# Two-layer attention block on Trainium2: at the layer boundaries, five tiles of squares summed by the matmul engine and the residual add moved to the vector engine

## The chip, the cores and the metric

The kernel runs on one core of one Trainium2 chip. The metric is device microseconds of one execution, as the median of several runs. A core has a matmul engine (TensorE, PE in the profile), a vector engine (VectorE, DVE), an activation engine (ScalarE, ACT), a general-purpose engine (GpSimd, POOL), a sequencer that issues most transfers (SyncE, SP), and DMA engines. Each engine works through its own queue in order, and waits on semaphores for the others.

## The reference, cut to what matters

Two layers work on a residual stream `x` of 512 tokens by 1024 channels. The two places in a layer at which the stream is updated look like this:

```python
mixed = (gate[..., :D_MODEL] * y_nsa + gate[..., D_MODEL:] * y_sb) @ w_out
x = x + rms_norm(mixed, norm_g[1])
hf = rms_norm(x, norm_g[2])
ff = jnp.square(jax.nn.relu(hf @ w_ff1)) @ w_ff2
return x + rms_norm(ff, norm_g[3])
```

Each update needs the sum of squares of the branch's result over all 1024 channels, then the residual add, then the sum of squares of the new `x` for the norm ahead of the next matrix.

## The kernel before, in words

The stream is kept transposed: channels lie on the 128 partitions in eight tiles (`KT` = 8) and the 512 tokens lie along a row. Every f32 product is made of three passes over split operands (`three`, lines 183 to 187): high weight by high activation, high by low, low by high. A `Weight` (lines 145 to 177) is loaded by a transfer that SP issues, its high part is rounded off on ACT (`w_hi`, line 157) and the rest subtracted on POOL (`w_lo`, line 162). There are two buffers for raw weights and four for split ones, so a new split waits until PE has left an older weight.

The code around the change is `tail` (lines 242 to 337). It runs four times: after `w_out` and after the second feed-forward matrix in each layer. In three of these a next matrix follows (`nxt` is set); these are the boundaries of this text, called 1, 2 and 3 in order of time. The fourth is the end of the kernel. At a boundary the tokens are cut in two halves of 256 (`HALVES`).

- The first three tiles of the result have been made and their squares summed over the whole row before `tail` starts. The last five (`GN` = 5) are made in `tail`, first for half 0, then for half 1 (`products`, `evacuate`).
- `evacuate` copies a product out of PSUM on DVE (line 261, or line 263 where a partial sum is added), squares it on ACT into a buffer `sq`, and adds the square on DVE to the accumulator `acc` (`sq_add`, lines 229 to 237; called `macc` or `facc` in the profile). `sq` has two buffers.
- `rstd_fin` (lines 209 to 222) multiplies `acc` with a matrix of ones on PE (line 212). This sums over partitions and leaves the sum on all of them (`ss`). ACT and DVE then make the reciprocal root (`Rpost`, or `Rpre` for the norm of the next matrix). The multiplication is f32, which the trace shows as two PE passes.
- `residual` (lines 282 to 296) handles the eight tiles: DVE scales a tile (`pn`, line 291), POOL adds the old `x` (line 292), ACT makes the high part `ah` of the next matrix's input and DVE the low part `al` (`xsplit`, lines 224 to 227).
- `squares` (lines 298 to 303) squares the new `x` on ACT and sums on DVE into `acc2`.
- `head_step` (lines 200 to 203) multiplies the new inputs with the next matrix's first four column tiles, one input tile after the other.

PE's order is the program's order. At a boundary it is: half 0 of the five tiles; tile 0 of half 1; `ss` of half 0; tiles 1 to 4 of half 1; `head_step` on half 0 for input tiles 0 and 1; `ss` of half 1; `head_step` on half 0 for tiles 2 to 7; `head_step` on half 1 for tiles 0 to 5; `ss` of the new `x`, half 0; tile 6; `ss` of the new `x`, half 1; tile 7; then the next stage. The order on the other engines is set when the program is built: a list scheduler takes, from the instructions that are ready by its own estimate of time, the one that comes first in the program. On the chip each queue then runs in that fixed order. In that program order `residual` of half 0 stands ahead of `evacuate` of the tiles 1 to 4 of half 1.

Of the kernel before, what the change touches and what calls it, by code (L numbers as in the profile page):

```python
# [8 lines left out]
F32 = mybir.dt.float32  # L9
F32R = mybir.dt.float32r  # L10
I32 = mybir.dt.int32
AF = mybir.ActivationFunctionType
ALU = mybir.AluOpType
# [12 lines left out]
P = 128  # L26
# [23 lines left out]
def layer_kernel(ctx, tc, xT, pos, gvec, tri, consts, smalls, w_in, w1, w_o, w_out, ff1, ff2, out):  # L50
    nc = tc.nc
    V, S, G, E = nc.vector, nc.scalar, nc.gpsimd, nc.tensor

    cp = ctx.enter_context(tc.tile_pool(name="cp", bufs=1))
    sp = ctx.enter_context(tc.tile_pool(name="sp", bufs=1))
# [6 lines left out]
    def big(tag, name, dt=F32):  # L62
        return sp.tile([P, T], dt, tag=tag, bufs=BUFS[tag], name=name)

    def half(name):
        return sp.tile([P, 256], F32, tag="sv", bufs=3, name=name)

    def psum(tag, name):
        return pp.tile([P, T], F32, tag=tag, bufs=2, name=name)
# [10 lines left out]
    x = [big("L", f"x{k}") for k in range(KT)]  # L80
# [8 lines left out]
    ones = cp.tile([P, P], F32, name="ones")  # L89
# [99 lines left out]
    def dense(ps, w, acts, k0=0):  # L189
        n = len(acts)  # L190
        for k in range(n):
            three(ps, w, k0 + k, acts[k], k == 0, k == n - 1)

    HALVES = (slice(0, 256), slice(256, 512))
    FULL = (slice(0, 512),)

    def cols(acts, c):
        return [(h[:, c], l[:, c]) for h, l in acts]

    def head_step(group, acts, c, ks):  # L200
        for k in ks:
            for ps, w in group:
                three(ps[:, c], w, k, (acts[k][0][:, c], acts[k][1][:, c]), k == 0, k == KT - 1)

    def gcol(l, n, k):
        c = (l * 4 + n) * KT + k
        return gv[:, c:c + 1]

    def rstd_fin(R, acc, c, more=None, tag="t"):
        n = c.stop - c.start  # L210
        ss = psum(tag, "ss")[:, 0:n]
        E.matmul(ss, ones, acc, start=True, stop=more is None)
        if more is not None:
            E.matmul(ss, ones, more, start=False, stop=True)
        v = half("var")
        y = R[:, c]
        S.activation(y, ss, AF.Ln, scale=1.0 / D, bias=eps_c)
        V.tensor_scalar(v, ss, 1.0 / D, EPS, ALU.mult, ALU.add)
        S.activation(y, y, AF.Exp, scale=-0.5)
        V.tensor_tensor(acc, y, y, ALU.mult)  # L220
        V.scalar_tensor_tensor(v, acc, -0.5, v, ALU.mult, ALU.mult)
        V.scalar_tensor_tensor(y, v, 1.5, y, ALU.add, ALU.mult)

    def xsplit(act, xk, g, c):
        h, l = act[0][:, c], act[1][:, c]
        S.activation(h, xk[:, c], AF.Copy, scale=g)
        V.scalar_tensor_tensor(l, xk[:, c], g, h.bitcast(F32), ALU.mult, ALU.subtract)

    def sq_add(acc, src, first, c, eng):
        n = c.stop - c.start  # L230
        if first:
            S.activation(acc, src, AF.Square)
        else:
            for o in range(0, n, 256):
                sq = sp.tile([P, 256], F32, tag="sq", bufs=2, name="sq")
                S.activation(sq, src[:, o:o + 256], AF.Square)
                eng.tensor_tensor(acc[:, o:o + 256], acc[:, o:o + 256], sq, ALU.add)

    def new_acts():
        return [(big("act", f"ah{k}", F32R), big("act", f"al{k}", F32R)) for k in range(KT)]  # L240

    def tail(l, n, mixed, acc, load, acts, prev, src, nxt, head):


        group = range(KT - GN, KT)
        last_sq = []
        na = new_acts() if nxt is not None else None
        R = big("R", "Rpost")
        R2 = big("R", "Rpre") if nxt is not None else None
        ws = [load(m, ("f", "w", "w", "w", "pt")[i]) for i, m in enumerate(group)]  # L250
        pst = [psum(("d", "s", "o", "o", "s")[i], f"tail{m}") for i, m in enumerate(group)]

        def products(hf, i):
            c = HALVES[hf]
            dense(pst[i][:, c], ws[i], cols(acts, c))

        def evacuate(hf, i):
            c = HALVES[hf]
            m, ps = group[i], pst[i][:, c]
            if prev is None:  # L260
                V.tensor_copy(mixed[m][:, c], ps)
            else:
                V.tensor_tensor(mixed[m][:, c], ps, prev[m][:, c], ALU.add)
            if nxt is None and (hf, i) == (1, GN - 1):
                last_sq.append(half("last_sq"))
                S.activation(last_sq[0], mixed[m][:, c], AF.Square)
            else:
                sq_add(acc[:, c], ps if prev is None else mixed[m][:, c], False, c, V)
            if nxt is None and hf == 1:
                S.activation(mixed[m][:, c], mixed[m][:, c], AF.Copy, scale=gcol(l, n, m))  # L270

        def old(hf):
            if src is None:
                return [x[k][:, HALVES[hf]] for k in range(KT)]
            r = []
            for j in range(4):
                t = big("sig", "x_old").rearrange("p (a t) -> p a t", a=2)
                nc.sync.dma_start(t, src[:, 2 * j:2 * j + 2, HALVES[hf]])
                r += [t[:, 0, :], t[:, 1, :]]
            return r  # L280

        def residual(hf, xo):
            c = HALVES[hf]
            for k in range(KT):
                t = big("t", "pn")[:, 0:256]
                if nxt is None and hf == 1:
                    e = G if k in ENDP else V
                    e.tensor_tensor(t, mixed[k][:, c], R[:, c], ALU.mult)
                    (G if k == 5 else e).tensor_tensor(x[k][:, c], t, xo[k], ALU.add)
                else:  # L290
                    V.scalar_tensor_tensor(t, mixed[k][:, c], gcol(l, n, k), R[:, c], ALU.mult, ALU.mult)  # L291
                    (V if nxt is None and k in (1, 4, 7) else G).tensor_tensor(x[k][:, c], t, xo[k], ALU.add)
                if nxt is not None:
                    xsplit(na[k], x[k], gcol(nxt[0], nxt[1], k), c)
                else:
                    nc.sync.dma_start(out[:, k, c], x[k][:, c])

        def squares(hf):
            c = HALVES[hf]
            acc2 = half("acc2")  # L300
            for k in range(KT):
                sq_add(acc2, x[k][:, c], k == 0, c, V)
            return acc2

        for i in range(GN):
            products(0, i)
            evacuate(0, i)
        xo = old(0)
        if src is not None:
            for k in range(KT):  # L310
                x[k] = big("L", f"x{k}")
        products(1, 0)
        rstd_fin(R, acc[:, HALVES[0]], HALVES[0])
        evacuate(1, 0)
        hd = head.start() if nxt is not None else None
        residual(0, xo)
        for i in range(1, GN):
            products(1, i)
            evacuate(1, i)
        xo = old(1)  # L320
        if nxt is None:
            for m in range(KT - GN):
                S.activation(mixed[m][:, HALVES[1]], mixed[m][:, HALVES[1]], AF.Copy, scale=gcol(l, n, m))
            rstd_fin(R, acc[:, HALVES[1]], HALVES[1], last_sq[0])
            residual(1, xo)
            return None
        head_step(hd, na, HALVES[0], (0, 1))
        rstd_fin(R, acc[:, HALVES[1]], HALVES[1])
        residual(1, xo)
        a2 = squares(0), squares(1)  # L330
        head_step(hd, na, HALVES[0], range(2, KT))
        head_step(hd, na, HALVES[1], range(PLAN["HS"]))
        rstd_fin(R2, a2[0], HALVES[0])
        head_step(hd, na, HALVES[1], range(PLAN["HS"], PLAN["HS2"]))
        rstd_fin(R2, a2[1], HALVES[1])
        head_step(hd, na, HALVES[1], range(PLAN["HS2"], KT))
        return na, R2, hd
# [118 lines left out]
    class Head:  # L456
# [5 lines left out]
        def load(self, sub=None, between=None):  # L462
            u = len(self.ws)
            self.ws.append(Weight(self.src[u], "P" if u < 3 else "w", sub, between))
# [6 lines left out]
    def layer(l, acts, R, heads):  # L471
# [498 lines left out]
        for m in range(KT - GN):  # L970
            ps = any_bank("wout")
            dense(ps, Weight(w_out[l, m]), merged)
            if m < 3:
                head.load()
            S.activation(mixed[m], ps, AF.Copy)
            sq_add(acc, mixed[m], m == 0, FULL[0], V)
# [46 lines left out]
    with tc.manual_schedule(engines={mybir.EngineType.PE}):  # L1023
        acts = new_acts()
        R = big("R", "R0")
        acc = big("st", "acc0")
# [16 lines left out]
        nxt = acts, R, hd  # L1043
        for l in range(DEPTH):
            nxt = layer(l, *nxt)
# [71 lines left out]
```

## Time and profile before

| what | us |
|---|---|
| median of 3 runs | 1628.49 (1623.24 to 1630.78) |
| profiled execution, its own time | 1626.38 |
| span of its trace | 1624.4 |
| PE busy | 1534.3 (94%) |
| DVE, ACT, POOL busy | 870.5, 747.9, 768.2 |

The span is what the profile sees from the first to the last instruction; the execution's own time is 2 us more. The median is another 2 us above that execution. PE is busy nearly all the time, so time is lost where PE waits, and a row for another engine matters where PE, or something PE waits for, stands behind it. Times in the rows are microseconds from the start of the span.

### The profile page before, as it was taken

The numbers are of one execution on the slowest core, as the hardware profiler recorded it, in microseconds if no ns is written. First come the engines' busy times: TensorE is split into PE (matmuls) and PEld (weight loads), VectorE is DVE, ScalarE is ACT, GpSimd is POOL, SyncE is SP. The second block draws the span as 40 slices with busy tenths as digits, with TensorE's granted clock in tenths as the row PEclk, the third lists the DMA queues.
The fourth block names the chain that finished last, engine by engine and source line by source line (L and its number), as shares of the span: only waits on it lengthen the run. The fifth ranks groups of instructions, "written<-read, shape, count | busy, mean of one in ns | idle before, by whom it ended". The sixth has DMA issues, their size and how long they took to land.

```text
span 1624.4 us, 20692 instructions
## 1 busy us (share of the span) xinstructions
PE 1534.3 (94%) x7810; PEld 1291.3 (79%) x7810; DVE 870.5 (54%) x1495; ACT 747.9 (46%) x1379; POOL 768.2 (47%) x527
## 2 busy tenths in 40 slices
PE   8788999999989999999887899999998999999996
PEld 5566778888988888888885777788878988888886
DVE  7877954354582332323799698534536823232245
ACT  6666755443352332324356677646343523232342
POOL 4762345446544444446546534354565344444452
PEclk9899999999999999999998999999999999999999
DMA  5464212224312322324234622122343133232321
GB/s 185 108 144 97 51 52 69 75 91 143 106 64 95 98 97 95 100 93 131 95 93 108 162 54 53 52 78 65 103 145 113 43 93 101 92 103 91 104 91 52
DMA packets 49331, 153.74 MB, mean 95 GB/s; under 512 B 5952, under 2 KB 12496, under 8 KB 49232
## 3 DMA queue, kind: packets, MB, share of 16 engines
q1 hardware_dynamic: 45888, 140.84, 27.2%
q0 software_dynamic: 3200, 11.55, 4.1%
q8 instruction: 61, 1.00, 0.3%
q14 instruction: 38, 0.31, 0.1%
q10 hardware_dynamic: 144, 0.03, 0.0%
HBM read 148.15 MB, written 4.26 MB: 94 GB/s over the span
## 4 chain that ended last, share of the span: by engine, by line
PE 77%; DVE 14%; ACT 3%; DMA 1%; issue 1%; POOL 0%; DVEq 0%; ACTq 0%; POOLq 0%
PE ff L186 12%; PE ff L185 12%; PE ff L187 12%; PE proj L483 5%; PE proj L479 5%; PE proj L481 5%; DVE P L690 2%; PE tail L187 2%; PE tail L186 2%; PE tail L185 2%; PE p_t L720 2%; DVE pn L291 2%; PE y L185 1%; PE y L187 1%; PE y L186 1%; PE head L185 1%
## 5 line engine op out<-in xcount | busy, mean ns | idle before, releaser
L162 POOL TENSOR_TENSOR w_lo<-w_raw,w_hi 128x1024 fp32r<-128x1024 f32 x204 | 496.7, 2435 | 503.2 <-ACT w_hi L157 483.5
L157 ACT ACTIVATE w_hi<-w_raw 128x1024 fp32r<-128x1024 f32 x226 | 239.1, 1059 | 530.0 <-PE ff L186 370.9
L483 PE MATMUL proj<-ah,w_lo 128*128 128x512 f32 x496 | 197.9, 399 | 1.7 <-POOL w_lo L162 1.7
L481 PE MATMUL proj<-al,w_hi 128*128 128x512 f32 x496 | 197.8, 399 | 0.0
L479 PE MATMUL proj<-ah,w_hi 128*128 128x512 f32 x496 | 196.8, 397 | 0.7 <-ACT w_hi L157 0.7
L185 PE MATMUL ff<-ah,w_hi 128*128 128x512 f32 x448 | 174.3, 389 | 0.0
L186 PE MATMUL ff<-al,w_hi 128*128 128x512 f32 x448 | 174.3, 389 | 0.0
L187 PE MATMUL ff<-ah,w_lo 128*128 128x512 f32 x448 | 174.3, 389 | 0.0
L186 PE MATMUL ff<-hl,w_hi 128*128 128x512 f32 x432 | 168.2, 389 | 0.8 <-DVE hl L181 0.8
L185 PE MATMUL ff<-hh,w_hi 128*128 128x512 f32 x432 | 168.1, 389 | 0.0
L187 PE MATMUL ff<-hh,w_lo 128*128 128x512 f32 x432 | 168.1, 389 | 0.0
L181 DVE TENSOR_TENSOR hl<-relu,hh 128x512 fp32r<-128x512 f32 x64 | 106.6, 1671 | 84.3 <-ACT hh L180 84.0
L483 PEld LDWEIGHTS proj<-ah,w_lo 128*128 128x128 f32 x496 | 94.1, 190 | 18.5 <-POOL w_lo L162 2.1
L479 PEld LDWEIGHTS proj<-ah,w_hi 128*128 128x128 f32 x496 | 94.0, 190 | 17.3 <-ACT w_hi L157 0.9
L481 PEld LDWEIGHTS proj<-al,w_hi 128*128 128x128 f32 x496 | 94.3, 190 | 16.7
L1012 DVE TENSOR_TENSOR ffa<-ff,ffa 128x512 f32<-128x512 f32 x38 | 26.3, 692 | 150.8 <-PE ff L187 150.8
L185 PEld LDWEIGHTS ff<-ah,w_hi 128*128 128x128 f32 x448 | 84.1, 188 | 17.5
L187 PEld LDWEIGHTS ff<-ah,w_lo 128*128 128x128 f32 x448 | 84.1, 188 | 17.5
L186 PEld LDWEIGHTS ff<-al,w_hi 128*128 128x128 f32 x448 | 84.1, 188 | 17.2
L186 PEld LDWEIGHTS ff<-hl,w_hi 128*128 128x128 f32 x432 | 81.1, 188 | 17.9 <-DVE hl L181 1.2
L185 PEld LDWEIGHTS ff<-hh,w_hi 128*128 128x128 f32 x432 | 81.1, 188 | 16.9
L187 PEld LDWEIGHTS ff<-hh,w_lo 128*128 128x128 f32 x432 | 81.1, 188 | 16.8
(311 smaller groups left out, 3431.1 us busy)
## 6 DMA issues: line engine op xcount, KB each, us to landing
w_raw<-in_ff_dram SPq DMA_DIRECT2D x128, 512.0 KB, 3.5
w_raw<-in_w_in_dram SPq DMA_DIRECT2D x69, 512.0 KB, 3.6
w_lo<-in_w_in_dram POOLq DMA_DIRECT2D x18, 512.0 KB, 7.5
w_raw<-in_w_dram SPq DMA_DIRECT2D x16, 512.0 KB, 3.5
w_raw<-in_w_o_dram SPq DMA_DIRECT2D x16, 512.0 KB, 3.5
w_raw<-in_w_out_dram SPq DMA_DIRECT2D x16, 512.0 KB, 3.5
x<-in_xT_dram SPq DMA_DIRECT2D x8, 256.0 KB, 6.5
w_lo<-in_w_dram POOLq DMA_DIRECT2D x4, 512.0 KB, 6.5
```

Source lines behind the costliest of these rows:

```text
L157: S.activation(h, raw, AF.Copy)
L162: (sub or G).tensor_tensor(l, raw, h.bitcast(F32), ALU.subtract)
L181: V.tensor_tensor(lo, src, hi.bitcast(F32), ALU.subtract)
L185: E.matmul(ps, w.hi(k), ah, start=first, stop=False)
L186: E.matmul(ps, w.hi(k), al, start=False, stop=False)
L187: return E.matmul(ps, w.lo(k), ah, start=False, stop=last)
L291: V.scalar_tensor_tensor(t, mixed[k][:, c], gcol(l, n, k), R[:, c], ALU.mult, ALU.mult)
L479: E.matmul(ps, w.hi(k), ah, start=(k == 0), stop=False)
L481: E.matmul(ps, w.hi(k), al, start=False, stop=False)
L483: E.matmul(ps, w.lo(k), ah, start=False, stop=(k == KT - 1))
L690: V.tensor_scalar(pr[h], pr[h], sm4[:, h:h + 1], None, ALU.mult)
L720: E.transpose(pt[:, P * h:P * h + P], pend[j][0][h][:, P * kt:P * kt + P], ident)
```

## The change

In the three boundaries `evacuate` no longer adds the squares of half 1 of the last five tiles to `acc`. The five squares are kept, and `rstd_fin` sums `acc` and then the five squares with six multiplications by ones into the same PSUM tile. The `sq` buffers go from two to five. The residual add of both halves moves from POOL to DVE in the three boundaries; in the fourth `tail` the engines stay as they were.

```diff
@@ rstd_fin
         E.matmul(ss, ones, acc, start=True, stop=more is None)
-        if more is not None:
-            E.matmul(ss, ones, more, start=False, stop=True)
+        for i, m in enumerate(more or ()):
+            E.matmul(ss, ones, m, start=False, stop=i == len(more) - 1)
@@ sq_add
-                sq = sp.tile([P, 256], F32, tag="sq", bufs=2, name="sq")
+                sq = sp.tile([P, 256], F32, tag="sq", bufs=5, name="sq")
@@ evacuate
             if nxt is None and (hf, i) == (1, GN - 1):
                 last_sq.append(half("last_sq"))
                 S.activation(last_sq[0], mixed[m][:, c], AF.Square)
+            elif nxt is not None and hf == 1:
+                last_sq.append(sp.tile([P, 256], F32, tag="sq", bufs=5, name="sq"))
+                S.activation(last_sq[-1], ps if prev is None else mixed[m][:, c], AF.Square)
             else:
                 sq_add(acc[:, c], ps if prev is None else mixed[m][:, c], False, c, V)
@@ residual
-                    (V if nxt is None and k in (1, 4, 7) else G).tensor_tensor(x[k][:, c], t, xo[k], ALU.add)
+                    (G if nxt is None and k not in (1, 4, 7) else V).tensor_tensor(x[k][:, c], t, xo[k], ALU.add)
@@ tail
-            rstd_fin(R, acc[:, HALVES[1]], HALVES[1], last_sq[0])
+            rstd_fin(R, acc[:, HALVES[1]], HALVES[1], last_sq)
...
-        rstd_fin(R, acc[:, HALVES[1]], HALVES[1])
+        rstd_fin(R, acc[:, HALVES[1]], HALVES[1], last_sq)
```

## Rows read from the trace of the kernel before

**Rows 1.** The page, busy time of each engine.

```profile
PE 1534.3 (94%) x7810; PEld 1291.3 (79%) x7810; DVE 870.5 (54%) x1495; ACT 747.9 (46%) x1379; POOL 768.2 (47%) x527
```

**Rows 2.** Waits of PE: waiter, releaser, us in total, times, longest.

```profile
PE ss L212 <- DVE macc L237: 8.2, 2, 4.1
...
PE head L186 <- DVE al L227: 7.1, 5, 1.9
PE ss L212 <- DVE facc L237: 5.7, 2, 4.9
```

**Rows 3.** PE at boundary 1: start, duration, line, tile, [idle before, releaser].

```profile
443.49 0.28 PE L185 MATMUL head<-ah,w_hi 128*128 128x256 f32 x1
443.61 0.28 PE L186 MATMUL head<-al,w_hi 128*128 128x256 f32 x1
...
447.11 0.39 PE L186 MATMUL head<-al,w_hi 128*128 128x256 f32 x1 [1.90 <-DVE al L227]
...
452.80 1.22 PE L212 MATMUL ss<-macc,ones 128*128 128x256 f32 x2 [4.12 <-DVE macc L237]
...
455.93 0.28 PE L186 MATMUL head<-al,w_hi 128*128 128x256 f32 x1
...
471.99 0.60 PE L212 MATMUL ss<-acc,ones 128*128 128x256 f32 x2
...
472.54 0.28 PE L186 MATMUL head<-al,w_hi 128*128 128x256 f32 x1
...
473.85 0.60 PE L212 MATMUL ss<-acc,ones 128*128 128x256 f32 x2
```

**Rows 4.** PE at boundaries 2 and 3, the same wait.

```profile
814.26 1.22 PE L212 MATMUL ss<-facc,ones 128*128 128x256 f32 x2 [4.93 <-DVE facc L237]
...
1257.25 1.22 PE L212 MATMUL ss<-macc,ones 128*128 128x256 f32 x2 [4.12 <-DVE macc L237]
```

**Rows 5.** Two stretches at boundary 1: length, busy PE, PEld, DVE, ACT, POOL, PEclk, DMA, GB/s.

```profile
448.50:452.80 4.30, 0.18 (x2) 0.00 (x0) 4.25 (x6) 0.73 (x4) 3.32 (x2) 0.56 0.37 114
452.80:455.80 3.00, 3.00 (x12) 2.82 (x13) 2.12 (x6) 2.67 (x7) 0.00 (x0) 0.50 0.56 180
```

**Rows 6.** DVE at boundary 1, order of time.

```profile
435.05 0.42 DVE L261 COPY mix<-tail 128x256 f32<-128x256 f32 x1 [0.35 <-PE tail L187]
435.39 4.30 DVE L291 SCALAR_TENSOR_TENSOR pn<-mix,gv,Rpost 128x256 f32<-128x256 f32 x4
...
443.18 2.40 DVE L237 TENSOR_TENSOR macc<-macc,sq 128x256 f32<-128x256 f32 x1 [0.51 <-ACT sq L236]
...
449.85 0.41 DVE L261 COPY mix<-tail 128x256 f32<-128x256 f32 x1
450.19 2.23 DVE L227 SCALAR_TENSOR_TENSOR al<-x,gv,ah 128x256 fp32r<-128x256 f32 x1
452.33 0.41 DVE L237 TENSOR_TENSOR macc<-macc,sq 128x256 f32<-128x256 f32 x1
...
456.70 0.42 DVE L222 SCALAR_TENSOR_TENSOR Rpost<-var,Rpost 128x256 f32<-128x256 f32 x1
...
469.66 2.53 DVE L237 TENSOR_TENSOR acc<-acc,sq 128x256 f32<-128x256 f32 x5
```

**Rows 7.** POOL at boundary 1, the first and last of three weight splits.

```profile
436.82 2.59 POOL L162 TENSOR_TENSOR w_lo<-w_raw,w_hi 128x1024 fp32r<-128x1024 f32 x1
...
449.61 2.52 POOL L162 TENSOR_TENSOR w_lo<-w_raw,w_hi 128x1024 fp32r<-128x1024 f32 x1
```

**Rows 8.** ACT, the last square of half 1 at boundary 1.

```profile
450.36 0.38 ACT L236 ACTIVATE sq<-tail 128x256 f32<-128x256 f32 x1 [1.83 <-DVE mix L261]
```

**Rows 9.** Instructions on pn: duration min/median/max in ns, starts, forms.

```profile
L291 DVE SCALAR_TENSOR_TENSOR pn<-mix,gv,Rpost x32: 471/954/2631, 435.4 to 1269.4; 128x256 f32<-128x256 f32 x32
L292 POOL TENSOR_TENSOR x<-pn,x_old x32: 721/917/928, 436.0 to 1270.5; 128x256 f32<-128x256 f32 x32
...
L292 DVE TENSOR_TENSOR x<-pn,x x3: 409/411/954, 1605.1 to 1609.4; 128x256 f32<-128x256 f32 x3
```

## The prediction, made before the changed kernel ran

> **What bounds the kernel now.** I read the page's busy times first. PE is busy 94% of the span [rows 1], so only PE's own waits can be won back, and added PE work costs its full time unless it lies in such a wait. Then PE's list of waits: DVE's additions of squares hold `ss` for 8.2 us and 5.7 us in all, and `al` holds the head products for 7.1 us [rows 2]. The timeline of PE puts these at the three boundaries. In boundary 1 PE starts the head products at 443.49, waits 1.90 us for `al`, then 4.12 us for the last square added to `macc`, and starts `ss` at 452.80 [rows 3]. The wait is 4.93 us in boundary 2 and 4.12 us in boundary 3 [rows 4]. [...] One `ss` and ten products take 3.13 us there, from 452.80 to 455.93; a product at full clock starts 0.12 us after the one before [rows 3]. An `ss` at full clock: 471.99 to 472.54, 0.55 us, holds one product besides, so 0.43 us [rows 3]. At full clock the eleven would be 0.43 + 1.20 = 1.63, so the clock costs 1.5 us.
>
> All in all boundary 1 takes 28.50 us from 443.49 to the next `ss` at 471.99 [rows 3]. The work between is 168 products and one `ss`: 168 x 0.12 + 0.43 = 20.6. So 7.9 us are lost there.
>
> Why is the last square so late? PE has finished the last tile at 443.49. DVE copies it out only at 449.85 [rows 3, 6], since its queue is behind. Two instructions show by what: an addition of 0.41 us takes 2.40 us at 443.18 [rows 6], and four `pn` take 4.30 us instead of about 1.6. POOL runs `w_lo` splits of 2.4 to 2.6 us and residual adds of 0.92 us meanwhile [rows 7, 9]. [...] The copy from PSUM takes 0.41 us all the same [rows 6].
>
> **The change, part by part.** *Added on PE:* five `ss` in each boundary, 5 x 0.43 = 2.15 us, 6.5 us in three. In the kernel before PE arrives at `ss` at 443.49 + 24 x 0.12 = 446.4 if `al` is in time, and waits until 452.8. The sums of `acc` and of the first squares run in that wait. Only the last, 0.43 us, must follow the last square. If the wait went away altogether, all 2.15 us would show. The best case of boundary 1 is so 7.9 - 2.15 = 5.75 us; with 0.8 us more in boundary 2, three give 18.
>
> *Removed on DVE:* the five additions, and with them what lay between the last square and `ss`. The last square starts at 450.36 [rows 8] and lasts 0.38, but `al` (2.23 us, held by a split) and the addition stand in front of `ss`, so it starts at 452.80 instead of about 450.8 [rows 6]. That is 2 us won if the last copy stays where it is.
>
> *Moved to DVE:* 48 residual adds (eight in each of two halves, three boundaries). One takes 0.41 us on DVE against 0.92 on POOL [rows 9]. By starts, the copy at 449.85 and the next instruction at 450.19 lie 0.34 us apart [rows 6]; I take 0.34 for an add and, as `pn` is 0.06 us longer [rows 9], 0.40 for `pn` and `al`. A tile then costs 0.40 + 0.34 + 0.40 = 1.14 us of DVE. POOL loses 0.92 us a tile, which now holds DVE up no longer.
>
> *Where the copies end up.* In program order the residual of half 0 stands ahead of the copies of half 1. Before, DVE ran out of ready residual work while POOL added, and the copies got in between. Now DVE always has a residual instruction ready, so I expect the copies of the last three tiles behind nearly all 24 of them. From 435.39 [rows 6] that is 8 x 1.14 + 3 x 0.34 = 10.1 us without POOL, to 445.5. Three splits start between 436.82 and 449.61 [rows 7]; nothing in the change removes one, and POOL, being free, can only start them sooner. If two of them stand in front of the last copy and each holds DVE for 2.40 - 0.41 = 2.0 us, it ends at 449.5; if three do, for all of 2.4 us, at 452.7. Before it ended at 450.26. I take 451.3, near the middle, as the third split starts about when DVE gets to its last tiles and I cannot tell which comes first. [...]
>
> *Sum.* From the end of the copy to the end of its square is 450.36 + 0.38 - 450.26 = 0.48 us, then 0.06 to the start of `ss`, then 0.43: 451.3 + 0.97 = 452.3. Before, the products that follow would, at full clock, have had to start at 455.93 - 10 x 0.12 = 454.7 to be where they were. That is 2.4 us won if the clock stays up, and 0.9 if it falls as before (1.5 us). PE again waits some 3 us in pieces, so I take 1.5 us. Three boundaries and the 0.8 of boundary 2 give 5.3 us. The ends: last copy at 449.5, clock up, 4.2 us each and 13.5 in all; last copy at 452.7, clock down, 0.4 us lost each, about 0.5 us slower in all with the 0.8 counted.
>
> *The 1.90 us wait for `al`* goes, but is worth nothing by itself: PE gets to `ss` sooner and waits there.
>
> *After `ss`.* `Rpost` of half 1 is ready at 457.12 [rows 6], 3.2 us after `ss`. Then DVE owes 9.1 us of residual and 14 additions of new squares, 4.8 us: 17.1 us after `ss`. PE comes to the second `ss` of the new `x` after 156 products and an `ss`, 19.1 us. So 2 us are spare; before it was 473.85 - 472.19 = 1.7 [rows 3, 6]. I cost this at nothing. The `sq` buffers: five squares now hold all five until PE reads them, so new squares of `x` other than the first wait for `ss`; they are not needed within 17 us of it. *Transfers:* no issue is added. SP's loads of the old `x` of half 1 wait for the adds of half 0, which come no later than before by more than 2 us, while their data are wanted after 457.
>
> The sum is against the profiled execution, 1626.4: 1621.1. The median stands 2.1 us above it: 1623.2.
>
> **Rivals.** *A, the copies come in time.* If DVE's queue has gaps, or the splits fall behind the copies, the last copy is made soon after 443.49 and PE never waits: 18 us less, 1610. For: without POOL DVE needs only 10.1 us where it had 14.9. Against: program order, and the splits.
>
> *B, three splits in front of the copy, and the clock falls.* The wait is as long as before and 1628.5 stands: the change then doesn't shorten the wait that it is about. For: the splits need ACT and a freed buffer only, and both are there by the middle of the stretch. Against: two `al` fewer would do.
>
> *C, slower: the second half becomes DVE's.* The place is the second `ss` of the new `x`. It decides when a split, or two, falls into the 17 us after `ss`: 4.8 us against 2.0 spare, 2.8 us late in each boundary, 8.4 in three, and with nothing won in front 1637. For: these adds used to run beside DVE. Against: the last of the splits starts at 449.61 [rows 7], as the four split buffers are then full until the head products end, and the change gives no fifth.
>
> **How the numbers follow.** The forecast gets 0.50, A 0.20, B 0.20, C 0.10. About 0.5% (8.1 us) is what a measurement of this kernel can tell from no change. Faster by more: A, and the third of the forecast's span of 0.5 us slower to 13.5 faster that lies beyond 8.1 us, 0.20 + 0.17 = 0.37. Slower by more: C but for its small end, 0.09. The rest, 0.54, is the same. The range goes from 1611, which leaves out the best of A, to 1633, which takes in B with its noise and leaves out most of C.
>
> **What would show it.** Right: PE's first wait for `al` is gone, `ss` of half 1 has six pairs of passes with gaps between the late ones, released by ACT squares, the last at 451 to 453 by the times of before; the last copy stands behind `al` of tile 5 or later in DVE's queue, with one or two instructions of 2 us or more ahead of it, beside `w_lo`. Wrong: the last copy before 446 (A), an idle PE ahead of the second `ss` of the new `x` (C), or `pn`, add and `al` of a tile costing DVE well over 1.14 us away from POOL's splits.

## The result, and the profile after

The changed kernel takes 1615.37 us (median of 6 runs, 1613.14 to 1618.03) against 1627.09 (6 runs, 1623.03 to 1630.78) of the kernel before, 11.7 us less: ratio 0.9934, 95% interval [0.9917, 0.9951]. (The quotient of the two medians is 0.9928; the kernels below are compared by the ratio.) Forecast were 5.3 us less. The profiled execution took 1615.27 us with a span of 1613.5; the span of before was 1624.4, so 10.9 us have to be found.

The page first: busy time of each engine, to be held against [rows 1].

```profile
PE 1539.8 (95%) x7840; PEld 1296.0 (80%) x7840; DVE 861.8 (53%) x1528; ACT 744.1 (46%) x1379; POOL 726.4 (45%) x479
```

PE has 30 more instructions (three boundaries, five sums of two passes) and 5.5 us more work, and the kernel is faster all the same. POOL lost the 48 residual adds. One of PE's waits (waiter, releaser, us in total, times, longest) shows where the room came from:

```profile
PE ss L214 <- ACT sq L269: 3.3, 2, 1.6
```

The 8.2 and 5.7 us of `ss` behind DVE's additions [rows 2] have become these 3.3 us behind ACT's squares, and 0.7 us behind an addition in boundary 2. Next boundary 1 on PE (start, duration, line, tile, [idle before, releaser]), from `ss` of half 0 to the last `ss` of the new `x`; the time between these two starts is called the length of a boundary from here on. The second fence has the one row of the kernel before that this needs and [rows 3] lack.

```profile
434.82 0.60 PE L212 MATMUL ss<-macc,ones 128*128 128x256 f32 x2
...
446.76 0.28 PE L185 MATMUL head<-ah,w_hi 128*128 128x256 f32 x1
...
449.79 0.60 PE L212 MATMUL ss<-macc,ones 128*128 128x256 f32 x2
450.23 1.89 PE L214 MATMUL ss<-sq,ones 128*128 128x256 f32 x8
453.75 0.70 PE L214 MATMUL ss<-sq,ones 128*128 128x256 f32 x2 [1.63 <-ACT sq L269]
...
473.41 0.60 PE L212 MATMUL ss<-acc,ones 128*128 128x256 f32 x2
```

```profile
431.55 0.60 PE L212 MATMUL ss<-macc,ones 128*128 128x256 f32 x2
```

The length was 473.85 [rows 3] - 431.55 = 42.30 us and is 473.41 - 434.82 = 38.59. Both waits of [rows 3], 1.90 and 4.12 us, have given way to one of 1.63: four of the five added sums run ahead of it, and the next product starts 0.34 us after the last. The wait and what follows by windows (length, busy PE, PEld, DVE, ACT, POOL, granted clock, DMA share, GB/s):

```profile
452.10:453.70 1.60, 0.02 (x1) 0.00 (x0) 1.60 (x4) 0.39 (x2) 0.56 (x1) 1.00 0.46 103
453.70:457.00 3.30, 3.25 (x25) 3.21 (x26) 2.27 (x7) 2.78 (x9) 0.00 (x0) 1.00 0.41 151
```

The granted clock is 1.00 in the wait and behind it; before the change it was 0.56 in the wait and 0.50 behind it [rows 5]. DVE and POOL at the same boundary:

```profile
439.84 3.31 DVE L295 TENSOR_TENSOR x<-pn,x_old 128x256 f32<-128x256 f32 x4
...
443.79 2.61 DVE L294 SCALAR_TENSOR_TENSOR pn<-mix,gv,Rpost 128x256 f32<-128x256 f32 x1
...
450.37 2.57 DVE L227 SCALAR_TENSOR_TENSOR al<-x,gv,ah 128x256 fp32r<-128x256 f32 x1
452.86 0.41 DVE L261 COPY mix<-tail 128x256 f32<-128x256 f32 x1
453.20 1.26 DVE L227 SCALAR_TENSOR_TENSOR al<-x,gv,ah 128x256 fp32r<-128x256 f32 x3
```

```profile
443.71 2.41 POOL L162 TENSOR_TENSOR w_lo<-w_raw,w_hi 128x1024 fp32r<-128x1024 f32 x1 [1.86 <-ACT w_hi L157]
449.63 3.03 POOL L162 TENSOR_TENSOR w_lo<-w_raw,w_hi 128x1024 fp32r<-128x1024 f32 x1 [3.50 <-ACT w_hi L157]
```

So DVE's queue is nearly as late as it was: the last copy comes 452.86 - 446.76 = 6.10 us after PE's first head product; before it was 449.85 - 443.49 = 6.36 [rows 3, 6]. What changed is what PE does until then, and that no addition follows the square. Boundary 3 looks the same (a wait of 1.64, 38.58 us long). In boundary 2 the wait is another: two splits in a row (801.92, 4.89 us of POOL) hold the first `al` (804.53, 2.56 us; the next, at 808.14, takes 0.47), and PE waits for it with the sums still to come.

```profile
807.14 0.58 PE L186 MATMUL head<-al,w_hi 128*128 128x256 f32 x1 [2.56 <-DVE al L227]
811.33 0.60 PE L212 MATMUL ss<-facc,ones 128*128 128x256 f32 x2
811.76 2.32 PE L214 MATMUL ss<-sq,ones 128*128 128x256 f32 x10
```

All six sums then run without a wait, and the boundary is 40.69 us long instead of 43.26.

The balance of the 10.9 us: boundaries 42.30 - 38.59 = 3.71, 43.26 - 40.69 = 2.57 and 42.78 - 38.58 = 4.20 us, 10.5 won. At the kernel's start, which the prediction did not look at, 5.6 us are lost: `ss` of the first `x` starts at 31.86 and not at 26.30. The stretches between, which the change does not edit, are shorter by 6.0 (2.3 from the first `ss` to boundary 1, 4.2 from boundary 2 to 3, 0.5 longer in the two others).

The 4.2 us are not chance scatter. From boundary 2 to 3 the six kernels of the table below that sum all five squares on PE take 396.3 to 397.9 us, and the four that do not take 399.5 to 405.6. Some 40 us ahead of boundary 3, in the products `y`, PE waits for DVE; the waits, and the 10 us from their ends, first before, then after:

```profile
1195.23 0.47 PE L185 MATMUL y<-onh,w_hi 128*128 128x512 f32 x1 [2.24 <-DVE sig L955]
1195.23:1205.23 10.00, 10.00 (x37) 8.10 (x38) 5.44 (x6) 3.36 (x5) 6.54 (x5) 0.83 0.61 202
```

```profile
1190.23 0.47 PE L185 MATMUL y<-onh,w_hi 128*128 128x512 f32 x1 [0.85 <-DVE sig L958]
1190.23:1200.23 10.00, 10.00 (x44) 8.31 (x45) 6.74 (x7) 4.62 (x6) 6.96 (x5) 1.00 0.63 209
```

In the four kernels the wait is 2.1 to 2.5 us and the clock behind it 0.83 or 0.84; in the six it is 0.9 to 1.1 us and 1.00. By these rows it is 1.4 us of wait and about 1.7 us of clock, so some 3 of the 4.2 us (an estimate). What DVE waits for begins with a load of `w_out`: ACT rounds off that weight before it splits the operand that DVE needs. The transfers in the 5 us from this load's issue, 1185.55 to 1190.55 before and 1181.93 to 1186.93 after (queue: packets, MB, share; then the load, with the us from issue to landing):

```profile
q8 instruction: 1, 0.02, 1.4%
w_raw<-in_w_out_dram SPq DMA_DIRECT2D x1, 512.0 KB, 4.8
```

```profile
w_raw<-in_w_out_dram SPq DMA_DIRECT2D x1, 512.0 KB, 3.4
```

In each of the four kernels one packet of instructions is moved while the load is on its way, and the load lands 4.6 to 5.0 us after its issue. In none of the six is there one, and it lands after 3.4 to 3.7 us. That the packet delays the load is argued from these ten traces; no run moved the packet alone. If it does, this part of the gain hangs on where the code's packets fall, and not on the boundaries. The stretch from the first `ss` to boundary 1 lasts 399.4 to 407.9 us over the ten kernels and follows no edit that I can see; its 2.3 us stay open.

### The profile page after: what moved, and what is told of

Read it like the earlier page. It is cut to its first block, busy times and chain, and to the rows that moved or that the text cites. A ratio compares the mean times of both kernels' runs of the same rounds, so it can differ in the third digit from the quotient of the medians.

```text
span 1613.5 us, 20715 instructions
## 1 busy us (share of the span) xinstructions
PE 1539.8 (95%) x7840; PEld 1296.0 (80%) x7840; DVE 861.8 (53%) x1528; ACT 744.1 (46%) x1379; POOL 726.4 (45%) x479
## 4 chain that ended last, share of the span: by engine, by line
PE 76%; DVE 13%; ACT 3%; DMA 2%; issue 2%; POOL 1%; DVEq 0%; ACTq 0%; POOLq 0%
PE ff L186 12%; PE ff L187 12%; PE ff L185 12%; PE proj L486 5%; PE proj L482 5%; PE proj L484 5%; DVE P L693 2%; PE tail L185 2%; PE tail L187 2%; PE tail L186 2%; PE p_t L723 2%; DMA w_raw<-in_w_in_dram 2%; PE y L185 1%; PE y L186 1%; PE y L187 1%
```

## The experiments

All lengths below in one table, for the ten kernels; each length is from one profiled execution. "First sum" is the start of the first `ss` in the kernel. The first four experiments ran on one chip and the last four on another, each group with its own runs of the kernel before (medians 1625.60 and 1626.03), so times of different groups are compared by their ratios.

| kernel | first sum | b. 1 | b. 2 | b. 3 | median us | ratio, interval |
|---|---|---|---|---|---|---|
| before | 26.30 | 42.30 | 43.26 | 42.78 | 1627.09 | |
| after | 31.86 | 38.59 | 40.69 | 38.58 | 1615.37 | 0.9934 [0.9917, 0.9951] |
| five buffers alone | 30.23 | 43.32 | 43.79 | 42.49 | 1631.91 | 1.0026 [1.0004, 1.0048] |
| PE sum and buffers | 30.18 | 38.63 | 39.61 | 38.62 | 1616.52 | 0.9942 [0.9924, 0.9960] |
| add on DVE alone | 26.61 | 42.26 | 42.97 | 43.57 | 1628.21 | 1.0014 [0.9996, 1.0031] |
| after, own buffers | 27.24 | 38.99 | 41.50 | 39.01 | 1613.65 | 0.9927 [0.9902, 0.9953] |
| last square alone | 26.92 | 40.89 | 42.69 | 41.04 | 1622.26 | 0.9966 [0.9948, 0.9984] |
| PE sum, own buffers | 26.75 | 38.05 | 39.23 | 38.04 | 1610.14 | 0.9907 [0.9883, 0.9931] |
| sums reversed | 30.45 | 42.40 | 43.26 | 42.42 | 1626.42 | 1.0000 [0.9983, 1.0017] |
| no POOL splits | 26.81 | 36.56 | 39.23 | 36.57 | 1607.13 | 0.9888 [0.9866, 0.9909] |

### The three parts alone

The change has three edits: more `sq` buffers, the sums on PE, the residual add on DVE. The first experiment is the kernel before with five buffers.

```diff
-                sq = sp.tile([P, 256], F32, tag="sq", bufs=2, name="sq")
+                sq = sp.tile([P, 256], F32, tag="sq", bufs=5, name="sq")
```

> The kernel before with five sq buffers in place of two, nothing else. Theory: in the changed kernel's trace the first sum of squares (start of the program) comes at 31.86 us instead of 26.30, and the change touches that place with nothing but the buffer count; so the buffers alone cost about 5.5 us there, and the three boundaries stay as before (42.3, 43.3 and 42.8 us from the half-0 sum to the last sum of the new x). Expected 5 us slower than before, about 1632, first sum at 31 to 32 us. Rival: the 5.5 us at the start are a matter of that one execution (transfers landing late), then first sum at 26 to 27 and no change in time.

It is slower, 1.0026 with an interval that just leaves 1 out. The largest difference in its trace is at the start, where the first sum comes 3.9 us late (5.5 were expected); boundaries 1 and 2 are also 1.0 and 0.5 us longer. DVE at the start, first in the kernel before, where what a split (22.13, 2.39 us) holds is an instruction on the table `tabs` that takes 0.17 us at 20.57, and then with five buffers:

```profile
22.14 2.42 DVE L114 TENSOR_SCALAR tabs<-tabs 128x32 f32<-128x32 f32 x1
```

```profile
19.51 1.75 DVE L227 SCALAR_TENSOR_TENSOR al<-x,gv,ah 128x512 fp32r<-128x512 f32 x1
21.19 2.60 DVE L237 TENSOR_TENSOR acc<-acc,sq 128x256 f32<-128x256 f32 x1
23.80 0.74 DVE L227 SCALAR_TENSOR_TENSOR al<-x,gv,ah 128x512 fp32r<-128x512 f32 x1
```

With five buffers the scheduler put an addition between two `al`; it takes 2.60 us in place of 0.41 [rows 6] (in the changed kernel the same addition, 2.58 us at 21.32, stands beside a split: 20.81, 2.81 us). PE waits 1.57 us for the `al` ahead of it and 1.61 for the one behind it; the kernel before has neither wait:

```profile
21.32 0.50 PE L186 MATMUL head<-al,w_hi 128*128 128x512 f32 x1 [1.57 <-DVE al L227]
24.59 0.50 PE L186 MATMUL head<-al,w_hi 128*128 128x512 f32 x1 [1.61 <-DVE al L227]
```

A buffer count that nobody needed at that place changed the order of a queue. In the changed kernel the first sum comes another 1.6 us later; no run shows why.

The second experiment is the changed kernel with the add back where it was, so the sums on PE and the buffers are left.

```diff
-                    (G if nxt is None and k not in (1, 4, 7) else V).tensor_tensor(x[k][:, c], t, xo[k], ALU.add)
+                    (V if nxt is None and k in (1, 4, 7) else G).tensor_tensor(x[k][:, c], t, xo[k], ALU.add)
```

> PE sums the five squares, five buffers, but the residual's add stays on POOL. Theory: POOL's adds and DVE's instructions go on taking turns, so the last copy of half 1 comes as late as before (6.4 us after PE's last tile), and what is won is only the stretch between the last square and the sum, about 2 us a boundary, less the time of a fallen clock: 0.5 to 2 us a boundary against 3.5 for the whole change (3.7, 2.6, 4.2 in the trace). With 5.5 us lost at the start it is 0 to 4 us slower than before. Rival: the sum on PE is the whole gain, each boundary 3 to 4 us shorter, total as the changed kernel, 1615.

The theory failed and the rival held. The three boundaries are 3.67, 3.65 and 4.16 us shorter than before, 11.5 in all, 1.0 more than in the changed kernel, and the ratios of the two are the same within their intervals (0.9942 and 0.9934). DVE's instructions are drawn out as before: an `al`, a `pn` and an `al` from 446.28 on take 0.96, 0.95 and 0.95 us in place of 0.47, and in the kernel before three among POOL's four adds from 439.37 (3.56 us) took 0.95, 0.95 and 0.96. But the last copy came 4.48 us after the first head product (454.48 - 450.00), earlier than with the add on DVE (6.10) and not as late as before, so PE hardly waits for the last square:

```profile
455.36 0.70 PE L214 MATMUL ss<-sq,ones 128*128 128x256 f32 x2 [0.16 <-ACT sq L269]
```

The third is the kernel before with the add on DVE and nothing else.

```diff
-                    (V if nxt is None and k in (1, 4, 7) else G).tensor_tensor(x[k][:, c], t, xo[k], ALU.add)
+                    (G if nxt is None and k not in (1, 4, 7) else V).tensor_tensor(x[k][:, c], t, xo[k], ALU.add)
```

> The residual's add on DVE, two buffers, the squares still added on DVE. Theory: DVE is freed of POOL's adds but still owes five additions behind the copies; the last copy comes at about the changed kernel's place (6.1 us after PE's last tile), the last square is added some 1 to 2.5 us later, in the queue behind the last al of half 0, so PE waits 3 to 4 us in one piece. Expected 0 to 2 us a boundary won, 0 to 6 in all, nothing lost at the start: 1621 to 1627. Rival: the moved add is the whole gain, 3 to 4 us a boundary, 1616 or less.

Nothing is won: 1.0014 [0.9996, 1.0031]. The theory had seen some of this, though it expected a wait of 3 to 4 us. The first wait of PE is almost gone (0.23 in place of 1.90 us) and the second is 1.34 us longer, with the clock again low behind it (0.54):

```profile
440.30 0.39 PE L186 MATMUL head<-al,w_hi 128*128 128x256 f32 x1 [0.23 <-DVE al L227]
447.32 1.22 PE L212 MATMUL ss<-macc,ones 128*128 128x256 f32 x2 [5.46 <-DVE macc L237]
```

```profile
447.30:450.50 3.20, 3.18 (x13) 3.00 (x14) 1.39 (x4) 1.78 (x5) 0.00 (x0) 0.54 0.36 140
```

So the gain in the boundaries is that of the sums on PE alone: with them it is there without the moved add, and the moved add and the buffers, each alone, bring none.

### Buffers of their own

The changed kernel, with `sq` back at two buffers. Four of the kept squares get buffers that nothing else uses; the fifth takes one of the three half-row buffers (`half`) that `rstd_fin` and `squares` also use.

```diff
-                sq = sp.tile([P, 256], F32, tag="sq", bufs=5, name="sq")
+                sq = sp.tile([P, 256], F32, tag="sq", bufs=2, name="sq")
...
-                last_sq.append(sp.tile([P, 256], F32, tag="sq", bufs=5, name="sq"))
+                last_sq.append(half("lsq") if i == GN - 1 else sp.tile([P, 256], F32, tag="lsq", bufs=4, name="lsq"))
```

> The changed kernel with the five kept squares in buffers of their own (four new ones and one of the sv tag), and the sq tag back at two. Theory: the start is as before (first sum at 26 to 27 us instead of 31.9) and the boundaries keep their gain, so it is about 5 us faster than the changed kernel: 1610 (0.990 of before). Rival: the five sq buffers also help the boundaries (new squares of x run ahead) or the stages between, and what is won at the start is lost there, 1615.

The first sum is back at 27.24, but the boundaries are 0.4 to 0.8 us longer. The time, 1613.65, lies 1.7 us under the changed kernel's, with the runs of both mixed, and not at the expected 1610. The same edit with the add on POOL is the sixth experiment:

> The changed kernel with the residual's sum back on POOL, and with buffers of their own for the five squares, so that the squares of the first x have their two buffers as before. Theory (the PE sum is the whole gain, the moved sum is worth nothing, and the five buffers cost about 4 us at the start): boundaries of 38.6, 39.6 and 38.6 us, as with the sum on POOL and five buffers, and a first ss at 26.3 us in place of 30.2: 1611 to 1614 us, about 3 us under the changed kernel. Rival (the buffers at the start cost nothing on the whole, because the attention stages behind take up what the start loses): within 1 us of the same kernel with five shared buffers, 1616.

1610.14 us, ratio 0.9907, where the same kernel with shared buffers had 0.9942; that is 5.7 us of 1626. What becomes of the start's loss is not the same in the two pairs. With the add on POOL the first sum is 3.4 us sooner with own buffers and boundary 1 begins 4.0 sooner (434.05 against 438.06), as the theory had it. With the add on DVE the first sum is 4.6 us sooner and boundary 1 only 0.5 (434.37 against 434.82), as the rival had it: the stages behind the start take up the loss. So what the shared buffers cost in the end is not settled.

Two pairs now price the moved add with the sums on PE: 0.9934 against 0.9942 without it with shared buffers, 0.9927 against 0.9907 with own ones. In boundaries it costs 0.0, 1.1 and 0.0 us in the first pair and 0.9, 2.3 and 1.0 in the second. It is worth nothing at best.

### Is it the last link, or all five?

The kernel before, in which only the last of the five squares goes to PE; the other four are added on DVE.

```diff
-            if nxt is None and (hf, i) == (1, GN - 1):
+            if (hf, i) == (1, GN - 1):
...
-        rstd_fin(R, acc[:, HALVES[1]], HALVES[1])
+        rstd_fin(R, acc[:, HALVES[1]], HALVES[1], last_sq[0])
```

> The kernel before, with the last square of a boundary alone summed by PE; the other four are still added on DVE, the residual's sum stays on POOL, and there are two square buffers. This takes away the last link alone (last square, addition on DVE, sum), which was 2.0 us of boundary 1 before (450.74 to 452.80). Theory (the gain is that DVE's queue is rid of all five additions, and that the sums fill PE's wait): most of the 3.7 to 4.2 us that the PE sum won in boundaries 1 and 3 is not here; the last copy comes some 6.4 us after PE's last tile, as before, PE still waits in long pieces at a clock well under 1.00, and the boundaries shorten by 1 to 2 us each: 1621 to 1624 us. Rival (it was the last link alone): the boundaries come out as with all five squares on PE, at 38.6 us against 42.3 and 42.8, and the time at 1614 to 1617.

The boundaries shorten by 1.4, 0.6 and 1.7 us: a third of the gain, as the theory had it (boundary 2 a little less than its 1 to 2 us). Boundary 1 shows why it is no more (PE, then DVE, then windows):

```profile
446.47 0.28 PE L185 MATMUL head<-ah,w_hi 128*128 128x256 f32 x1
...
450.08 0.39 PE L186 MATMUL head<-al,w_hi 128*128 128x256 f32 x1 [1.89 <-DVE al L227]
...
452.10 1.22 PE L212 MATMUL ss<-macc,ones 128*128 128x256 f32 x2 [0.37 <-DVE macc L237]
453.71 1.22 PE L214 MATMUL ss<-last_sq,ones 128*128 128x256 f32 x2 [0.39 <-ACT last_sq L266]
```

```profile
446.15 2.40 DVE L237 TENSOR_TENSOR macc<-macc,sq 128x256 f32<-128x256 f32 x1 [0.51 <-ACT sq L236]
...
452.83 0.41 DVE L261 COPY mix<-tail 128x256 f32<-128x256 f32 x1
```

```profile
450.08:453.71 3.63, 2.87 (x13) 1.87 (x14) 3.63 (x7) 2.58 (x6) 2.85 (x3) 0.69 0.51 169
453.71:457.00 3.29, 3.29 (x13) 3.11 (x14) 3.29 (x6) 2.33 (x6) 1.41 (x1) 0.50 0.56 137
```

The first head product is at 446.47, so the last copy stands 6.36 us behind it, to the hundredth where it stood before. An addition of 2.40 us, after a wait of 0.51 for its square, is still in front of it, as at 443.18 in [rows 6]. The last sum starts 453.71 - 446.47 = 7.24 us after that product instead of 9.31, so the link that was taken away was worth 2.07 us. Of these 1.41 reach the end of the boundary: the products behind the sum still run at a granted clock of 0.50 up to 457.00.

### The same work in another order

The changed kernel with the six sums in reverse: the square that comes last is summed first. Each engine has the same work.

```diff
-        E.matmul(ss, ones, acc, start=True, stop=more is None)
-        for i, m in enumerate(more or ()):
-            E.matmul(ss, ones, m, start=False, stop=i == len(more) - 1)
+        terms = [acc, *(more or ())]
+        if rev:
+            terms.reverse()
+        for i, m in enumerate(terms):
+            E.matmul(ss, ones, m, start=i == 0, stop=i == len(terms) - 1)
...
-        rstd_fin(R, acc[:, HALVES[1]], HALVES[1], last_sq)
+        rstd_fin(R, acc[:, HALVES[1]], HALVES[1], last_sq, rev=True)
```

> The changed kernel with the six sums of a boundary's second half in reverse order: the last square first, the sum of the earlier ones last. The same work on every engine, but PE has nothing to do until the last square is there, and the five other sums (5 x 0.43 us = 2.15 us) run behind it. Theory (the early sums fill PE's wait, and the filled wait keeps the clock at 1.00): PE waits for the last square in one piece of about 3.8 us (1.63 + 2.15) in boundaries 1 and 3, the granted clock falls to 0.5 to 0.7 there, and these boundaries take 38.6 + 2.15 + about 1.5 for the clock = 42 us, almost the 42.3 and 42.8 of the kernel before; boundary 2, which waits for al and not for the last square, stays within 2.2 us: 1622 to 1626 us. Rival 1 (the filling counts, the clock does not fall): 40.7 us each and 1620. Rival 2 (only DVE's shorter queue counts): no change from the changed kernel's 1615.

The gain in the boundaries is gone: they are 0.10 us longer than before, the same, and 0.36 shorter. The time is that of before too, 1.0000 [0.9983, 1.0017], but by a balance: the first sum is 4.2 us late, with the five shared buffers, and the stretches that the edit does not touch are 4.1 us shorter. PE and the window behind the wait in boundary 1:

```profile
446.11 0.28 PE L185 MATMUL head<-ah,w_hi 128*128 128x256 f32 x1
...
453.07 3.67 PE L216 MATMUL ss<-sq,ones 128*128 128x256 f32 x10 [3.79 <-ACT sq L271]
456.54 1.06 PE L216 MATMUL ss<-macc,ones 128*128 128x256 f32 x2
457.03 0.70 PE L185 MATMUL head<-ah,w_hi 128*128 128x256 f32 x1
```

```profile
453.07:457.00 3.93, 3.93 (x12) 3.17 (x13) 0.71 (x2) 1.89 (x5) 0.00 (x0) 0.63 0.57 199
```

The last square is there 453.07 - 446.11 = 6.96 us after the first head product, against 453.75 - 446.76 = 6.99 in the changed kernel: DVE and ACT are as fast. Only PE's order differs. It waits 3.79 us in one piece, and the clock falls to 0.63 over the 3.9 us behind the wait. The six sums take 457.03 - 453.07 = 3.96 us; at full clock they would be 6 x 0.43 = 2.58, so the clock costs 1.4. With the five sums that no longer hide, 2.15, this is 3.5 of the 3.81 us by which boundary 1 is longer (42.40 against 38.59). Both halves of the theory are needed; rival 1, without the clock, had 40.7, and rival 2, by which only DVE's shorter queue counts, had no change. Boundary 2 lost its 2.57 us as well, where the theory allowed up to 2.2.

### Without the splits

The kernel with the sums on PE, own buffers and the add on POOL, with the low parts of three weights after boundaries 1 and 3 made by an accumulating DMA, a way that the kernel already uses elsewhere: ACT writes the negated weight in the rounded format, and a transfer that POOL issues adds the weight to it. Boundary 2 is left as it is.

```diff
-                dense(ps, Weight(ff1[l, c * KT + m]), acts)
+                dense(ps, Weight(ff1[l, c * KT + m], sub="dma" if c == 0 and m < 7 else None), acts)
```

> The kernel with the residual's sum on POOL and own square buffers, with three weight tiles after boundaries 1 and 3 (the first three of the first ff1 stage that POOL splits) split by an accumulating DMA in place of POOL, so that POOL runs no split while the boundary's copies are made; boundary 2 is left as it is, as a control. Theory (the splits hold DVE's instructions for 2 to 2.5 us, and so set when the last copy is made, but with the sums filling PE's wait that no longer decides): the last copy of boundary 1 comes 2 to 3 us sooner after PE's last tile than the 4.5 us of the kernel with the splits, DVE has no instruction of over 2 us there, and PE gains only what it still waits for in that kernel, under 1.7 us in each of the two boundaries; boundary 2 the same. 1609 to 1613 us, not told apart from the kernel with the splits. Rival (the splits are the bound): 3 us or more in each, 1605 to 1607. Against both: if the accumulating DMAs come late, PE waits for weights in the ff1 stage and the time is longer.

1607.13 us, the fastest of all. Boundary 1 on PE and DVE:

```profile
444.67 0.28 PE L185 MATMUL head<-ah,w_hi 128*128 128x256 f32 x1
...
447.55 0.60 PE L212 MATMUL ss<-macc,ones 128*128 128x256 f32 x2
447.98 2.32 PE L214 MATMUL ss<-lsq,ones 128*128 128x256 f32 x10
```

```profile
440.15 2.37 DVE L227 SCALAR_TENSOR_TENSOR al<-x,gv,ah 128x256 fp32r<-128x256 f32 x1
...
445.55 0.41 DVE L261 COPY mix<-tail 128x256 f32<-128x256 f32 x1
445.89 0.47 DVE L227 SCALAR_TENSOR_TENSOR al<-x,gv,ah 128x256 fp32r<-128x256 f32 x1
446.81 1.68 DVE L227 SCALAR_TENSOR_TENSOR al<-x,gv,ah 128x256 fp32r<-128x256 f32 x4 [0.45 <-ACT ah L226]
```

The last copy stands 0.88 us (445.55 - 444.67) behind the first head product instead of 4.5, PE has no wait at all in boundaries 1 and 3, and boundaries 1 and 3 are 1.49 and 1.47 us shorter than with the splits, boundary 2 the same to the hundredth. The expectation for the copy was too small (2 to 3 us sooner; it was 3.6), the one for PE right: a copy 3.6 us sooner wins 1.5, as PE had little left to wait for. One `al` of over 2 us is left, at 440.15, which the expectation had excluded; POOL issues one of the transfers there (439.89, 0.88 us) and makes two adds in a row (440.50, 1.74 us), and which of the two holds DVE was not tried. The next two issues, 1.77 us from 445.29, leave the `al` at 445.89 at 0.47, which speaks for the adds. The splits set the time of the copies; with the sums in the gap they cost PE no more than this. The fall in the median, 3.0 us, fits the 2 x 1.5, though the intervals of the two kernels overlap. The time itself, 1607.13, is nearer the rival's than the theory's; the boundaries decide for the theory, as the rival had 3 us or more in each. Against the kernel before, boundary 1 is 5.74 us shorter, and the prediction's best case for it was 5.75. No wait of PE for a `w_lo` shows up behind the boundaries, so the case against both did not come.

## Why the prediction was right, and where it was off

**The range held, and the sign of the likeliest case; its middle was 8 us too high.** The likeliest class, no more than 0.5% either way, was missed: 0.66% less was measured, with an interval that ends at 0.49%. (5.4 of the 14.0 us of the forecast's span lie beyond 8.1, which is 0.39 and not a third; the chance of a larger gain should have been 0.39 and not 0.37.) That the total is close to the 10.5 us of the boundaries is luck: the prediction had neither the 5.6 us lost at the start nor the 6.0 won in the stretches between, and they cancel. In boundary 1 the sum can be settled term by term. All of the following is in times of before, 446.76 - 443.49 = 3.27 us off those of after.

**The removed link (right).** It was put at 2 us if the copy stays; the kernel with the last square alone has the copy at the same place and the sum 2.07 us sooner.

**The last copy (late behind splits, as forecast; 1.3 us off).** Forecast to end at 451.3, between 449.5 and 452.7; it ended at 452.86 + 0.41 - 3.27 = 450.0. Three splits did stand in front of it, for which the forecast had 452.7, and two things make the difference. Three `al` of the eight came behind the copy, 3 x 0.40 = 1.2 us less. And the splits held DVE for 3.31 - 1.43 = 1.9 us (four adds, three at 0.34 and one at 0.41 without it), 2.61 - 0.47 = 2.1 and 2.57 - 0.47 = 2.1, 6.1 in all instead of 3 x 2.4 = 7.2, 1.1 less. That gives 450.4. No run shows a hold of 2.4 us, the term on which the 452.7 and the 4.8 us of rival C rest; in its place stand these 1.9 to 2.1. Three of the signs that were to show it right were narrowly missed: the copy stands behind the `al` of tile 4 and not of tile 5, three held instructions and not one or two stand ahead of it, and the last sum starts at 450.5 and not between 451 and 453.

**The clock (the step that failed).** The text said "PE again waits some 3 us in pieces, so I take 1.5 us", between 2.4 with the clock up and 0.9 with it down; the 1.5 us from one to the other are the 3.13 us from 452.80 on in boundary 1, at the granted 0.50 [rows 3, 5], less 1.63 at 1.00. PE waits 1.63 us, because the copy came sooner and four sums lie in the gap, and the granted clock is 1.00 throughout. The forecast let the sums run in the wait and still priced the clock by 3 us of waiting; in the reversed order, with the same work and a wait of 3.79 us, the clock does fall to 0.63. The sum of the parts then comes out: 1.5 + 0.9 for the clock + 1.3 for the copy = 3.7 us, and 3.71 were measured. In boundary 3 the same two terms and 0.5 that it had been longer than boundary 1 before (42.78 against 42.30) give 4.2, measured 4.20. Boundary 2 won 2.57 where 2.3 were forecast, with a wait of 2.56 us that no row had announced and a granted clock of 0.76 over the 7 us around it.

**The sums on PE (right, and undervalued).** That 2.15 us of sums run in the wait was the argument for costing only the last. But they were entered as a cost that is hidden. The reversed order shows that hiding them is the larger part: 3.8 us in boundaries 1 and 3 and 2.6 in boundary 2 hang on it, in boundary 1 2.15 of work and 1.4 of clock.

**The residual add on DVE (wrong by sign).** The forecast credited it with DVE being held up no longer. Alone it wins nothing, and with the sums on PE it makes the last copy later, 6.10 us behind the product instead of 4.48. A POOL add held a `pn` for about half a microsecond (0.95 us at 440.50 and 0.47 at 445.50 in the kernel before), and an add on DVE takes 0.34 to 0.41, so there was little to win.

**The `sq` buffers (missed).** They were costed at nothing, by their use in the boundaries, where that holds. The loss is at the start, in code that the diff reaches only by a shared name: 3.9 us later in the first sum with five buffers alone, 5.6 in the changed kernel. How much of it reaches the end is not settled.

**After `ss` (right).** No wait of PE appears ahead of the second `ss` of the new `x`, so rival C did not come. Rival A, PE never waiting, did not come either. In boundary 1 it came with the add left on POOL and the splits taken away; with the add on POOL and the splits there, `ss` waits 0.16 us. So the splits stood against it, as the prediction said, but so did the moved add. Rival B had the copy too late and the clock too low.

## What to carry to other kernels

Where an engine waits for the last of several pieces, let it take the earlier ones itself while it waits, and order the work so that the piece that comes last is taken last; the same work in the opposite order won nothing here. Price a wait of PE together with the clock behind it: here the granted clock was 1.00 behind the 1.63 us that were left of a filled wait, and 0.63 behind an unfilled one of 3.79. And when a diff changes a buffer count, look at every place that draws from that pool, since the order of a queue can change there, as at the start here (the first sum 3.9 us later with five buffers alone). Before a difference in an unedited stretch is called noise, set that stretch side by side over all kernels: here one of them followed the edit.

## What the runs showed of the hardware that was not expected

- A wait of 1.63 us after busy stretches left the granted clock at 1.00; waits of 3.79 us (reversed sums) and 5.46 us (add on DVE alone) were followed by 0.63 and 0.54. The wait of 2.56 us in boundary 2 lay in a stretch of 0.76 (804.30 to 811.30). The single waits of 2.1 to 2.5 us ahead of boundary 3 were followed by 0.83 or 0.84 over 10 us, those of 0.9 to 1.1 at the same place by 1.00.
- A load of 512 KB landed 4.6 to 5.0 us after its issue in the four kernels in which a packet of instructions was moved meanwhile, and 3.4 to 3.7 us after it in the six in which none was. Whether the packet is the cause was not tried.
- In the kernel without splits, with accumulating transfers in their place, the DMA engines were busy throughout the stretch below (share 1.01, and 1.08 in the 2.65 us behind it), and four `al` took 1.68 us together there (446.81, above), where the changed kernel's single one beside a split took 2.57. The `al` of 2.37 us at 440.15 stands beside POOL's own work, its adds or its issue.

```profile
444.67:447.55 2.88, 2.88 (x27) 2.88 (x26) 2.43 (x6) 2.72 (x8) 2.39 (x3) 1.00 1.01 325
```
